# A fast matrix product whose kept weight sum moves into the tiles of the norm's rows, with weight chunks fetched three ahead

## The chip, the cores and the metric

The kernel runs on one core of a Trainium2 chip. The metric is the device time of one execution in microseconds (us); the time before is the median of three runs.

## The reference, cut to what matters

Two layers of an encoder trunk over 512 rows of width 1024. Each layer is a mixer, a cross attention and a gated MLP, each with a residual and a layer norm behind it. The change touches the MLP's second product and the norm that follows it (DFF is 2816, ALPHA is 4 to the power 1/4):

```python
def conv_ffn(x, w_up, conv_w, conv_b, w_down):
    up = x @ w_up                                  # 512 x 1024 @ 1024 x 5632
    a, g = up[..., :D_FF], up[..., D_FF:]
    g = causal_dwconv(g, conv_w) + conv_b
    return (jax.nn.gelu(g) * a) @ w_down           # 512 x 2816 @ 2816 x 1024

x = layer_norm(alpha * x + conv_ffn(...), ln_ffn_g[layer], ln_ffn_b[layer])
```

## The kernel before, in words

**Numbers.** Every matrix product is made of three matmuls on 32-bit data split into a high and a low part (`mm3`, lines 218 to 222): high by high, high by low, low by high. So each weight chunk, 128 x 1024 numbers or 512 KB, goes through a chain: SP issues a DMA into a `raw` tile, ScalarE (ACT) casts it to the high part `wh` (line 85), VectorE (DVE) subtracts that to get the low part `wl` (line 86). These two instructions together are called a split.

**The weight stream.** `plan` lists all chunks in the order of use. `Weights.load` (line 184) first fetches until more than `AHEAD` chunks are fetched and not split, then splits the oldest. `proj_batch` and the products call `weights.done()` (a `load`) each time a chunk has been used. There are 7 `raw` tiles and 5 pairs of `wh` and `wl`. A tile framework places the instructions on the engines: each engine runs its own list in order, the lists are made by the framework's scheduler, and a tile's slot is handed on when its last reader is done. So SP issues DMAs in a fixed order, and a DMA whose `raw` slot is not free holds back all DMAs behind it.

**The MLP.** The 22 feature tiles of the hidden layer go in three groups of 8, 8 and 6 (`FFN_GROUPS`). For a group, `ffn_up` computes the hidden tiles, and then a product with the matching rows of `w_down` is added to the residual `xt`. The last group uses an ordinary product followed by the norm (`residual_norm`). The first two groups use `fast_product` (line 345), a Winograd form with 7 block products in place of 8. It needs sums of weight blocks, which POOL (GpSimd) makes while the chunks are fetched (`Weights.fast`, line 136). There are four fast products in the kernel: two groups in each of two layers.

**One fast product.** It runs over four pairs of rows, i = 0 to 3. In its first half TensorE (PE) uses, for each i, a chunk `b11b21` and half of a kept sum t1 (chunk `t1t1`, one for two i). In the second half it uses, for each i, a chunk `t2b22` and half of a kept sum t4 (chunk `t4t4`). At the end it uses the kept sums t3 (chunk `t3t3`). For a chunk `t2b22` SP fetches two `raw` tiles (rows of half 1, then of half 0 of `w_down`), and POOL runs three instructions of 128 x 512: line 162 makes t3 from the first, line 163 makes t2, line 164 makes t4. Here the four `t2b22` chunks of one product are called c0 to c3, and their two DMAs c0a and c0b to c3a and c3b. `t4t4` for c0 and c1 is T4a, that for c2 and c3 is T4b.

Line 164 is the last reader of the second `raw` tile of a chunk, so that tile's slot is free when line 164 is done.

**The tile `blocks`.** t3 of all four chunks is kept in a tile of 128 x 2048 from the pool `fpool`, which has one slot. The same slot holds the hidden blocks of `ffn_up` (`Blocks.new`, line 258), four of them one after the other in a group; each is read last by the split in `finish` (line 272). Only after the last of them can t3 be written.

**The accumulators.** In the fast product PE accumulates into X, Y and Z, two PSUM tiles each. After the first half DVE adds them to `xt` (line 354): X[0], X[1], Z[0], Z[1], Y[0], Y[1], and PE then goes on accumulating into X and Y. So PE's first matmul of the second half into Y[1] waits for the add of Y[1].

**The norm's rows.** `load_rows` (line 300) fetches gain and bias of the norm, spread over 128 partitions, into the tiles `grow` and `brow` (128 x 1024, one slot each) by a DMA on POOL's queue. `residual_norm` calls it first thing, so in the MLP the rows of `ln_ffn` lie in their tiles through all three groups.

Of the kernel before, what the change touches and what calls it, by code (L numbers as in the profile page):

```python
# [8 lines left out]
F32 = mybir.dt.float32  # L9
# [5 lines left out]
P = 128  # L15
S = 512
D = 1024
# [8 lines left out]
CH = 1024  # L26
# [1 line left out]
EPS = 1e-5  # L28
WINDOWS = (2, 4, 8, 16)
RING = 5  # L30
AHEAD = 2
FFN_GROUPS = ((0, 8), (8, 16), (16, 22))
PAD = 16

# [2 lines left out]
def kernel(ctx: ExitStack, tc: tile.TileContext, a: dict, out: bass.AP):  # L37
# [8 lines left out]
    gpool = ctx.enter_context(tc.tile_pool(name="gpool", bufs=1))  # L46
    tpool = ctx.enter_context(tc.tile_pool(name="tpool", bufs=4))
    fpool = ctx.enter_context(tc.tile_pool(name="fpool", bufs=1))
# [5 lines left out]
    def nm(s):  # L54
        uid[0] += 1
        return f"{s}{uid[0]}"

    def ps_tile():
        return pspool.tile([P, 512], F32, tag="ps", name=nm("ps"))
# [4 lines left out]
    def slot(dtype=F32R):  # L64

        return apool.tile([P, 2 * CH], dtype, tag="act", name=nm("act"))
# [9 lines left out]
    def raw_tile():  # L76
        return rpool.tile([P, CH], F32, tag="raw", name=nm("raw"))

    def blocks_tile():

        return fpool.tile([P, 2 * CH], F32, tag="blocks", name=nm("blocks"))

    def split(h, l, src):

        nc.scalar.copy(h, src)  # L85
        nc.vector.tensor_sub(l, src, h.bitcast(F32))  # L86
# [41 lines left out]
    class Weights:  # L128
# [7 lines left out]
        def fast(self, what, layer, i):  # L136

            w = a["ffn_w_down"][layer]
            half = [slice(0, 512), slice(512, CH)]

            def fetch(src):
                t = raw_tile()
                nc.sync.dma_start(t[:, : src.shape[-1]], src)
                return t

            def both(key):

                if i % 2 == 0:
                    self.kept[key] = raw_tile()
                return self.kept[key][:, half[i % 2]]  # L150

            if what == "b11b21":
                w0, w1 = fetch(w[0, i]), fetch(w[1, i][:, half[0]])
                nc.gpsimd.tensor_sub(both("t1"), w1[:, half[0]], w0[:, half[0]])  # L154
                return w0
            if what == "t2b22":
                w1, w0 = fetch(w[1, i]), fetch(w[0, i])
                if i % 4 == 0:
                    self.kept["t3"] = blocks_tile()
                t3 = self.kept["t3"][:, (i % 4) * 512 : (i % 4 + 1) * 512]  # L160
                b12 = t2 = w1[:, half[0]]
                nc.gpsimd.tensor_sub(t3, w1[:, half[1]], b12)  # L162
                nc.gpsimd.tensor_add(t2, t3, w0[:, half[0]])  # L163
                nc.gpsimd.tensor_sub(both("t4"), w0[:, half[1]], t2)  # L164
                return w1
            if what == "t3t3":
                return self.kept["t3"][:, (i % 4) * 512 : (i % 4 + 2) * 512]
            return self.kept.pop({"t1t1": "t1", "t4t4": "t4"}[what])

        def fetch(self):  # L170
            if self.loaded == len(plan):
# [12 lines left out]
        def load(self):  # L184
            while self.loaded < len(plan) and len(self.fetched) <= AHEAD:
                self.fetch()
            if self.fetched:
                raw = self.fetched.pop(0)
                w = duo("w")
                split(*(t[:, : raw.shape[-1]] for t in w), raw)  # L190
                self.ready.append(w)
# [56 lines left out]
    class Blocks:  # L248
# [8 lines left out]

        def new(self):

            f = blocks_tile().rearrange("p (b s) -> p b s", b=8)  # L260

            def finish():
                def sub(to, x, y, op=ALU.subtract):
                    nc.vector.tensor_tensor(f[:, to, :], f[:, x, :], f[:, y, :], op=op)

                sub(self.S1, self.A21, self.A22, ALU.add)
                sub(self.S2, self.S1, self.A11)
                sub(self.S3, self.A11, self.A21)
                sub(self.S4, self.A12, self.S2)
                h, l = (slot()[:, : 7 * 256].rearrange("p (b s) -> p b s", b=7) for _ in range(2))  # L270
                self.pairs.append((h, l))
                split(h, l, f[:, :7, :])

            return [f[:, self.A11 :: self.A21, :], f[:, self.A12 : self.A22 + 1, :]], finish
# [20 lines left out]
    def proj_tok(ps, act, k, t, w, kk, start, stop, cols=slice(0, 512)):  # L295
        c = slice(t * P, (t + 1) * P)
        wh, wl = (v[:, kk * 512 + cols.start : kk * 512 + cols.stop] for v in w)
        mm3(ps[:, cols], act.h(k)[:, c], act.l(k)[:, c], wh, wl, start, stop)

    def load_rows(name, layer, n, eng=nc.gpsimd):  # L300
        t = gpool.tile([P, D], F32, tag=name[-1:] + "row", name=nm("row"))
        eng.dma_start(t[:, :n], a[name][layer : layer + 1, :].to_broadcast([P, n]))
        return t[:, :n]

# [109 lines left out]
    def residual_norm(groups, wname, ln, layer, last=False, hooks={}, ahead=None):  # L414

        g, b = load_rows(f"{ln}_g", layer, D), load_rows(f"{ln}_b", layer, D)
        wi = min(layer, a[wname].shape[0] - 1)
        xT = None
        for gi, (make, k0, k1) in enumerate(groups):
            act = make()
            final = gi == len(groups) - 1
            nk = k1 - k0
            if isinstance(act, Blocks):
                fast_product(act, layer, k0 // 2, gi == 0)
                continue  # L430

            def add(t, c, ps):
                z = xt[t][:, c]
                nc.vector.scalar_tensor_tensor(z, z, ALPHA if gi == 0 else 1.0, ps, op0=ALU.mult, op1=ALU.add)


            cut = [256 if last and t == NT - 1 else 512 for t in range(NT)]
            stats = [spool.tile([P, 4, 6], F32, tag="stats", name=nm("stats")) for _ in range(NT)] if final else None

            def stat(t, c0, c1):  # L440
                for c in range(c0, c1, cut[t]):
                    nc.vector.bn_stats(stats[t][:, c // cut[t], :], xt[t][:, c : c + cut[t]])

            for n in range(2):
                if n == 0 or not final:
                    ps = [ps_tile() for _ in range(NT)]
                    for k in range(nk):
                        if gi == 0 and n == 0 and k in hooks:
                            hooks[k]()
                        if k % 2 == 0:  # L450
                            c = weights.take(wname, wi, n, (k0 + k) // 2)
                        for t in range(NT):
                            proj_tok(ps[t], act, k, t, c, k % 2, k == 0, k == nk - 1)
                        if k % 2:
                            weights.done()
                    for t in range(NT):
                        add(t, slice(n * 512, (n + 1) * 512), ps[t])
                        if final:
                            stat(t, 0, 512)
                    continue  # L460
                chunks = [weights.take(wname, wi, n, (k0 + k) // 2) for k in range(0, nk, 2)]
                xT = None if last else Act(KD)
                if ahead:
                    ahead()
                for t in range(NT):
                    for c in range(0, 512, cut[t]):
                        ps = ps_tile()
                        for k in range(nk):
                            if k == 2 and c == 0 and t in (2, 3) and not last:
                                to_feat(xT, t - 2)  # L470
                            proj_tok(ps, act, k, t, chunks[k // 2], k % 2, k == 0, k == nk - 1, slice(c, c + cut[t]))
                        add(t, slice(512 + c, 512 + c + cut[t]), ps[:, c : c + cut[t]])
                        stat(t, 512 + c, 512 + c + cut[t])
                    normalise(xt[t], stats[t][:, : D // cut[t], :], g, b, (out[0, t * P : (t + 1) * P, :] if last else None))
                weights.done(len(chunks))

        def late():
            to_feat(xT, NT - 2)
            to_feat(xT, NT - 1)

        return xT, late


    def mixer_ab(xT):
# [3 lines left out]
        for k in range(KD):  # L488
# [4 lines left out]
            if k % 2:  # L493
                weights.done()
        g, b = load_rows("sgu_ln_g", 0, AW, nc.sync), load_rows("sgu_ln_b", 0, AW, nc.sync)
        for t in range(NT):
            nc.scalar.activation(v[t], ps[t], AF.Gelu_apprx_tanh)
# [314 lines left out]
```

## Time and profile before

| what | value |
|---|---|
| median of 3 runs | 1358.01 us (1357.94 to 1358.12) |
| the profiled execution, its own time | 1357.58 us |
| its span (first to last instruction) | 1355.8 us |
| mean granted TensorE clock | 0.998 of full speed |
| PE busy | 1329.4 us, 98% |
| DVE, ACT, POOL busy | 826.3, 496.9, 151.1 us |

The execution takes 1.8 us more than its span, and 0.43 us less than the median. A busy PE is not PE at its peak: a matmul of 512 columns is shown with 0.39 us, but the next one starts 0.23 us after it. Lost time of PE is therefore read from the starts of its matmuls.

### The profile page before, as it was taken

The page shows a single profiled execution, that of the slowest core. Times are in us where ns is not written, and L with a number is a line of the kernel's source. Part 1 is how long each engine was busy: PE and PEld are TensorE (multiplying, and loading weights), DVE is VectorE, ACT ScalarE, POOL GpSimd, SP SyncE. Part 2 cuts the span into 40 slices and gives each one's busy share as a digit, 9 for nine tenths or more (in the row PEclk, how much of TensorE's full clock was granted, in tenths as well). Part 3 has the DMA queues.
Part 4 walks back from the last instruction along what each step waited for, and adds up shares of the span by engine and source line. Part 5 has one row for each costly group of instructions (what it writes and reads, how often), then busy time and mean ns, then how long its engine had stood idle before and what let it go on. Part 6 is the DMA issues. An engine that isn't in the chain of part 4 may idle for free.

```text
span 1355.8 us, 16402 instructions
## 1 busy us (share of the span) xinstructions
PE 1329.4 (98%) x6526; PEld 1124.3 (83%) x6526; DVE 826.3 (61%) x1102; ACT 496.9 (37%) x671; POOL 151.1 (11%) x132
## 2 busy tenths in 40 slices
PE   8999999999999999999999999999999999999997
PEld 7888888898878887888988888988898878887886
DVE  6668446676566656547744447565676665557446
ACT  5343445235333333332522222354243333334330
POOL 0102000010150005000100001000111050213001
PEclk9999999999999999999999999999999999999999
DMA  9543533223244225433633331542152353226201
GB/s 342 181 125 98 172 120 124 62 94 109 94 162 149 86 88 181 128 95 107 202 94 97 105 94 47 159 152 78 47 156 81 104 178 120 82 92 215 94 0 63
DMA packets 47454, 161.88 MB, mean 119 GB/s; under 512 B 5648, under 2 KB 5776, under 8 KB 47376
## 3 DMA queue, kind: packets, MB, share of 16 engines
q1 hardware_dynamic: 45648, 154.53, 35.6%
q0 software_dynamic: 1728, 6.29, 1.5%
q8 instruction: 51, 0.84, 0.3%
q14 instruction: 27, 0.22, 0.1%
HBM read 158.70 MB, written 2.10 MB: 119 GB/s over the span
## 4 chain that ended last, share of the span: by engine, by line
PE 83%; issue 8%; POOL 5%; DMA 2%; DVE 1%; ACT 1%; POOLq 0%; DVEq 0%; SPq 0%
PE ps L220 27%; PE ps L221 27%; PE ps L222 27%; DMA raw<-in_ffn_w_down 2%; POOL blocks L162 2%; POOL raw L163 1%; PE ps L339 1%; POOL raw L164 1%; ACT wh L85 1%; PE ps L659 1%; POOL raw L154 0%; DVE wl L86 0%; POOL rs L311 0%; DVE x L314 0%; PE ps L536 0%
## 5 line engine op out<-in xcount | busy, mean ns | idle before, releaser
L86 DVE TENSOR_TENSOR wl<-raw,wh 128x1024 fp32r<-128x1024 f32 (+1 forms) x267 | 332.2, 1244 | 319.1 <-ACT wh L85 310.9
L85 ACT CAST wh<-raw 128x1024 fp32r<-128x1024 f32 (+1 forms) x267 | 279.0, 1045 | 551.0 <-PE ps L221 265.4
L220 PE MATMUL ps<-act,wh 128*128 128x512 f32 (+1 forms) x1316 | 478.5, 364 | 0.0
L221 PE MATMUL ps<-act,wh 128*128 128x512 f32 (+1 forms) x1316 | 478.1, 363 | 0.0
L222 PE MATMUL ps<-act,wl 128*128 128x512 f32 (+1 forms) x1316 | 478.0, 363 | 0.0
L221 PEld LDWEIGHTS ps<-act,wh 128*128 128x128 f32 x1316 | 248.4, 189 | 38.9
L220 PEld LDWEIGHTS ps<-act,wh 128*128 128x128 f32 x1316 | 248.3, 189 | 38.8
L222 PEld LDWEIGHTS ps<-act,wl 128*128 128x128 f32 x1316 | 248.3, 189 | 38.7
L220 PE MATMUL ps<-wh,act 128*128 128x512 f32 (+1 forms) x678 | 264.3, 392 | 10.6 <-DVE x L354 5.7
L221 PE MATMUL ps<-wl,act 128*128 128x512 f32 (+1 forms) x678 | 263.9, 389 | 5.9 <-DVE wl L86 5.9
L222 PE MATMUL ps<-wh,act 128*128 128x512 f32 (+1 forms) x678 | 263.6, 389 | 0.0
L220 PEld LDWEIGHTS ps<-wh,act 128*128 128x128 f32 x678 | 127.6, 189 | 39.2 <-DVE x L354 7.3
L221 PEld LDWEIGHTS ps<-wl,act 128*128 128x128 f32 x678 | 127.9, 189 | 33.8 <-DVE wl L86 8.1
L222 PEld LDWEIGHTS ps<-wh,act 128*128 128x128 f32 x678 | 127.7, 188 | 26.1
L311 POOL TENSOR_TENSOR rs<-rs,mhalf 128x1 f32<-128x1 f32 x28 | 39.9, 1427 | 808.5 <-DVE rs L310 808.5
L85 ACT CAST act<-ps 128x256 fp32r<-128x256 f32 (+1 forms) x144 | 62.9, 470 | 120.3 <-PE ps L339 79.2
L86 DVE TENSOR_TENSOR act<-ps,act 128x256 fp32r<-128x256 f32 (+1 forms) x144 | 73.0, 535 | 13.4 <-ACT act L85 13.0
L563 DVE SCALAR_TENSOR_TENSOR tmp<-ps,convw,tmp 128x511 f32<-128x511 f32 x88 | 65.6, 746 | 1.5
L700 ACT ACTIVATE tmp<-tmp 128x512 f32<-128x512 f32 x44 | 27.9, 633 | 96.9 <-DVE tmp L563 96.7
L154 POOL TENSOR_TENSOR raw<-raw,raw 128x512 f32<-128x512 f32 x16 | 26.0, 1625 | 254.7 <-DVE wl L86 202.8
L705 DVE TENSOR_TENSOR blocks<-tmp,ps 128x512 f32<-128x512 f32 x32 | 22.0, 687 | 46.3 <-PE ps L222 40.3
L86 DVE TENSOR_TENSOR act<-blocks,act 128x1792 fp32r<-128x1792 f32 x16 | 33.5, 2092 | 22.6 <-ACT act L85 22.6
(77 smaller groups left out, 778.8 us busy)
## 6 DMA issues: line engine op xcount, KB each, us to landing
raw<-in_ffn_w_up SPq DMA_DIRECT2D x88, 512.0 KB, 3.8
raw<-in_ffn_w_down SPq DMA_DIRECT2D x60, 512.0 KB, 3.5
raw<-in_c_w_in SPq DMA_DIRECT2D x24, 512.0 KB, 3.6
raw<-in_xa_wk SPq DMA_DIRECT2D x16, 512.0 KB, 3.7
raw<-in_xa_wq SPq DMA_DIRECT2D x16, 512.0 KB, 4.0
raw<-in_xa_wv SPq DMA_DIRECT2D x16, 512.0 KB, 3.6
raw<-in_xa_wo SPq DMA_DIRECT2D x16, 512.0 KB, 4.4
raw<-in_ab_w_f SPq DMA_DIRECT2D x8, 512.0 KB, 6.9
```

Source lines behind the costliest of these rows:

```text
L85: nc.scalar.copy(h, src)
L86: nc.vector.tensor_sub(l, src, h.bitcast(F32))
L154: nc.gpsimd.tensor_sub(both("t1"), w1[:, half[0]], w0[:, half[0]])
L162: nc.gpsimd.tensor_sub(t3, w1[:, half[1]], b12)
L163: nc.gpsimd.tensor_add(t2, t3, w0[:, half[0]])
L220: nc.tensor.matmul(ps, lh, rh, start=start, stop=False, skip_group_check=more)
L221: nc.tensor.matmul(ps, lh, rl, start=False, stop=False, skip_group_check=more)
L222: nc.tensor.matmul(ps, ll, rh, start=False, stop=stop, skip_group_check=more)
L311: nc.gpsimd.tensor_tensor(rs, rs, mhalf, op=ALU.pow)
L563: nc.vector.scalar_tensor_tensor(dst[:, s:], src[:, : S - s], tap(2 - s), dst[:, s:], op0=ALU.mult, op1=ALU.add)
L700: nc.scalar.activation(g, g, AF.Gelu_apprx_tanh)
L705: nc.vector.tensor_mul(to[m % 2], *halves)
```

## The change

It has three parts. (1) t3 is kept in row tiles: c0 and c1 in one of them (`grow`), c2 and c3 in the other (`brow`); the tile `blocks` is left to the hidden blocks. (2) `load_rows` moves from the head of `residual_norm` to the last group, behind `ffn_up`, since the row tiles hold t3 until then; where there is one group only, the place is the same. (3) `AHEAD` is 3 in place of 2.

```diff
-AHEAD = 2
+AHEAD = 3
...
-    def blocks_tile():
-        return fpool.tile([P, 2 * CH], F32, tag="blocks", name=nm("blocks"))
+    def row_tile(tag):
+        return gpool.tile([P, D], F32, tag=tag + "row", name=nm("row"))
...
             if what == "t2b22":
                 w1, w0 = fetch(w[1, i]), fetch(w[0, i])
-                if i % 4 == 0:
-                    self.kept["t3"] = blocks_tile()
-                t3 = self.kept["t3"][:, (i % 4) * 512 : (i % 4 + 1) * 512]
+                if i % 2 == 0:
+                    self.kept["t3", i // 2] = row_tile("gb"[i // 2 % 2])
+                t3 = self.kept["t3", i // 2][:, half[i % 2]]
...
-            if what == "t3t3":
-                return self.kept["t3"][:, (i % 4) * 512 : (i % 4 + 2) * 512]
-            return self.kept.pop({"t1t1": "t1", "t4t4": "t4"}[what])
+            return self.kept.pop({"t1t1": "t1", "t4t4": "t4", "t3t3": ("t3", i // 2)}[what])
...
-            f = blocks_tile().rearrange("p (b s) -> p b s", b=8)
+            f = fpool.tile([P, 8, 256], F32, tag="blocks", name=nm("blocks"))
...
     def load_rows(name, layer, n, eng=nc.gpsimd):
-        t = gpool.tile([P, D], F32, tag=name[-1:] + "row", name=nm("row"))
+        t = row_tile(name[-1:])
...
-        g, b = load_rows(f"{ln}_g", layer, D), load_rows(f"{ln}_b", layer, D)
         wi = min(layer, a[wname].shape[0] - 1)
         xT = None
         for gi, (make, k0, k1) in enumerate(groups):
...
                 fast_product(act, layer, k0 // 2, gi == 0)
                 continue
+            if final:
+                g, b = load_rows(f"{ln}_g", layer, D), load_rows(f"{ln}_b", layer, D)
```

The scheduler decides where the instructions stand. DVE, around the turn from the first to the second half of the first fast product, before: the splits are those of c0 (`raw_3186`), c1 (`raw_3237`), T4a (`raw_3193`), c2 (`raw_3270`), c3 (`raw_3300`) and T4b (`raw_3276`); the rows with `x_113` to `x_116` are the adds, the last one (`ps_3216`) that of Y[1].

```order
L86 TENSOR_TENSOR wl_3267<-raw_3186,wh_3266 128x1024
L354 SCALAR_TENSOR_TENSOR x_113<-x_113,ps_3217 128x512
L354 SCALAR_TENSOR_TENSOR x_114<-x_114,ps_3218 128x512
L354 SCALAR_TENSOR_TENSOR x_113<-x_113,ps_3213 128x512
L354 SCALAR_TENSOR_TENSOR x_114<-x_114,ps_3214 128x512
L86 TENSOR_TENSOR wl_3279<-raw_3237,wh_3278 128x1024
L86 TENSOR_TENSOR wl_3308<-raw_3193,wh_3307 128x1024
L354 SCALAR_TENSOR_TENSOR x_115<-x_115,ps_3215 128x512
L86 TENSOR_TENSOR wl_3330<-raw_3270,wh_3329 128x1024
L354 SCALAR_TENSOR_TENSOR x_116<-x_116,ps_3216 128x512
L86 TENSOR_TENSOR wl_3334<-raw_3300,wh_3333 128x1024
L86 TENSOR_TENSOR wl_3364<-raw_3276,wh_3363 128x1024
```

DVE at the same place in the changed kernel, where c0 to c3 are `raw_3154`, `raw_3191`, `raw_3262`, `raw_3275`, T4a is `raw_3161`, T4b is `raw_3269`, and Y[1] is `ps_3219`:

```order
L86 TENSOR_TENSOR wl_3272<-raw_3154,wh_3271 128x1024
L86 TENSOR_TENSOR wl_3283<-raw_3191,wh_3282 128x1024
L86 TENSOR_TENSOR wl_3305<-raw_3161,wh_3304 128x1024
L352 SCALAR_TENSOR_TENSOR x_113<-x_113,ps_3220 128x512
L352 SCALAR_TENSOR_TENSOR x_114<-x_114,ps_3221 128x512
L352 SCALAR_TENSOR_TENSOR x_113<-x_113,ps_3216 128x512
L352 SCALAR_TENSOR_TENSOR x_114<-x_114,ps_3217 128x512
L352 SCALAR_TENSOR_TENSOR x_115<-x_115,ps_3218 128x512
L86 TENSOR_TENSOR wl_3327<-raw_3262,wh_3326 128x1024
L86 TENSOR_TENSOR wl_3331<-raw_3275,wh_3330 128x1024
L352 SCALAR_TENSOR_TENSOR x_116<-x_116,ps_3219 128x512
L86 TENSOR_TENSOR wl_3363<-raw_3269,wh_3362 128x1024
```

The splits of c1 and T4a moved ahead of all six adds, and the add of Y[1], which stood behind the split of c2, now stands behind that of c3.

SP, the eight DMAs of c0 to c3 of the first fast product with the engines whose semaphores each waits for, before (DMAHW are semaphores of earlier DMAs):

```order
L143 DMA raw_3186<-in_ffn_w_down 128x1024 [waits DMAHW5_49,DMAHW4_49,Pool_49]
L143 DMA raw_3188<-in_ffn_w_down 128x1024 [waits DVE_49]
L143 DMA raw_3237<-in_ffn_w_down 128x1024 [waits DMAHW7_49,DVE_49]
L143 DMA raw_3239<-in_ffn_w_down 128x1024 [waits DMAHW1_49,DVE_49]
L143 DMA raw_3270<-in_ffn_w_down 128x1024 [waits DMAHW3_49,DVE_49]
L143 DMA raw_3272<-in_ffn_w_down 128x1024 [waits DVE_49]
L143 DMA raw_3300<-in_ffn_w_down 128x1024 [waits DMAHW5_49,DVE_49,Pool_49]
L143 DMA raw_3302<-in_ffn_w_down 128x1024 [waits DMAHW0_49,Pool_49]
```

SP at the same place in the changed kernel:

```order
L143 DMA raw_3154<-in_ffn_w_down 128x1024 [waits DMAHW5_49,DMAHW4_49,Pool_49]
L143 DMA raw_3156<-in_ffn_w_down 128x1024 [waits DVE_49]
L143 DMA raw_3191<-in_ffn_w_down 128x1024 [waits DMAHW7_49,DMAHW6_49,Pool_49]
L143 DMA raw_3193<-in_ffn_w_down 128x1024 [waits DVE_49]
L143 DMA raw_3262<-in_ffn_w_down 128x1024 [waits DMAHW1_49,DMAHW0_49,Pool_49]
L143 DMA raw_3264<-in_ffn_w_down 128x1024 [waits DVE_49]
L143 DMA raw_3275<-in_ffn_w_down 128x1024 [waits DMAHW3_49,DMAHW2_49,Pool_49]
L143 DMA raw_3277<-in_ffn_w_down 128x1024 [waits DVE_49]
```

c1a and c2a waited for a DVE split and now wait for POOL. In the built program c1a has the slot that c0b gives back, c2a that of c1b, and c3a that of c2b: each waits for line 164 of the chunk before it. c1b, c2b and c3b wait for the splits of the first kept t1, of the `b11b21` chunk i = 2, and of the second t1.

## Rows read from the trace of the kernel before

**Rows 1.** The page: busy time of the engines in us, with the share of the span and the instructions.

```profile
PE 1329.4 (98%) x6526; PEld 1124.3 (83%) x6526; DVE 826.3 (61%) x1102; ACT 496.9 (37%) x671; POOL 151.1 (11%) x132
```

**Rows 2.** The waits of PE over the whole span, its two rows that do not belong to the start: line, whom it waited for, us in total, times, longest us.

```profile
PE ps L221 <- DVE wl L86: 5.9, 4, 1.5
PE ps L220 <- DVE x L354: 5.7, 4, 1.4
```

**Rows 3.** The timeline of PE at the turn of the first fast product: start, us, line, what, and idle time before with its releaser.

```profile
392.96 0.39 PE L222 MATMUL ps<-wh,act 128*128 128x512 f32 x1
393.42 0.73 PE L220 MATMUL ps<-wh,act 128*128 128x512 f32 x2
395.64 0.50 PE L221 MATMUL ps<-wl,act 128*128 128x512 f32 x1 [1.48 <-DVE wl L86]
395.98 0.40 PE L222 MATMUL ps<-wh,act 128*128 128x512 f32 x1
...
398.04 0.39 PE L220 MATMUL ps<-wh,act 128*128 128x512 f32 x1
399.84 0.50 PE L220 MATMUL ps<-wh,act 128*128 128x512 f32 x1 [1.42 <-DVE x L354]
400.19 0.40 PE L221 MATMUL ps<-wl,act 128*128 128x512 f32 x1
...
401.82 0.39 PE L220 MATMUL ps<-wh,act 128*128 128x512 f32 x1
```

**Rows 4.** Busy time of the engines in one stretch of 58 us at each of the four fast products, the first and the last of the four, in the order PE, weight loads, DVE, ACT, POOL, with the granted clock and the share of the DMA engines.

```profile
347.00:405.00 58.00, 55.02 (x240) 44.57 (x239) 33.63 (x37) 21.77 (x23) 20.66 (x14) 1.00 0.40 124
...
1177.00:1235.00 58.00, 55.03 (x241) 44.56 (x240) 33.52 (x37) 21.63 (x22) 20.80 (x14) 1.00 0.37 124
```

**Rows 5.** The waits of all engines over the whole span, one row of them.

```profile
POOL blocks L162 <- DVE act L86: 115.0, 4, 28.9
```

**Rows 6.** The timeline of POOL in the first fast product: lines 162 and 163 for c0, and line 163 for c2.

```profile
383.27 1.29 POOL L162 TENSOR_TENSOR blocks<-raw 128x512 f32<-128x512 f32 x1 [28.70 <-DVE act L86]
384.64 1.29 POOL L163 TENSOR_TENSOR raw<-blocks,raw 128x512 f32<-128x512 f32 x1
...
394.58 2.15 POOL L163 TENSOR_TENSOR raw<-blocks,raw 128x512 f32<-128x512 f32 x1
```

**Rows 7.** The timeline of ACT at the same place: the cast of c2.

```profile
396.77 1.05 ACT L85 CAST wh<-raw 128x1024 fp32r<-128x1024 f32 x1 [3.40 <-POOL raw L163]
```

**Rows 8.** The timeline of DVE in the first fast product: splits of hidden blocks (1792 columns), splits of chunks (1024 columns) and adds.

```profile
358.85 2.03 DVE L86 TENSOR_TENSOR act<-blocks,act 128x1792 fp32r<-128x1792 f32 x1 [1.76 <-ACT act L85]
365.96 1.22 DVE L86 TENSOR_TENSOR wl<-raw,wh 128x1024 fp32r<-128x1024 f32 x1
371.12 1.22 DVE L86 TENSOR_TENSOR wl<-raw,wh 128x1024 fp32r<-128x1024 f32 x1 [3.95 <-ACT wh L85]
379.57 1.22 DVE L86 TENSOR_TENSOR wl<-raw,wh 128x1024 fp32r<-128x1024 f32 x1 [0.71 <-ACT wh L85]
381.16 2.03 DVE L86 TENSOR_TENSOR act<-blocks,act 128x1792 fp32r<-128x1792 f32 x1 [0.37 <-ACT act L85]
397.85 1.34 DVE L86 TENSOR_TENSOR wl<-raw,wh 128x1024 fp32r<-128x1024 f32 x1 [1.67 <-ACT wh L85]
399.11 0.68 DVE L354 SCALAR_TENSOR_TENSOR x<-x,ps 128x512 f32<-128x512 f32 x1
```

**Rows 9.** The timeline of SP: the issues of c0a, c0b and c3a, and from the view of their line the time from issue to landing of the eight DMAs of c0 to c3 (first) and of the eight that follow them in a burst (second).

```profile
354.59 0.33 SPq L143 DMA_DIRECT2D raw<-in_ffn_w_down  x1
356.32 0.33 SPq L143 DMA_DIRECT2D raw<-in_ffn_w_down  x1
388.45 0.33 SPq L143 DMA_DIRECT2D raw<-in_ffn_w_down  x1
DMA to landing us min/median/max: 3.4/3.6/4.5
DMA to landing us min/median/max: 3.6/4.7/5.7
```

**Rows 10.** The timeline of DVE and POOL at one place in the first `ffn_up`, where the two work at the same time.

```profile
339.04 2.31 DVE L86 TENSOR_TENSOR wl<-raw,wh 128x1024 fp32r<-128x1024 f32 x1
337.18 3.09 POOL L154 TENSOR_TENSOR raw<-raw,raw 128x512 f32<-128x512 f32 x1 [6.97 <-DMA raw<-in_ffn_w_down]
```

**Rows 11.** The timeline of PE at the end of the first half: its last matmul with the `b11b21` chunk i = 3, and its last with the second t1.

```profile
390.24 0.39 PE L222 MATMUL ps<-wh,act 128*128 128x512 f32 x1
391.60 0.39 PE L222 MATMUL ps<-wh,act 128*128 128x512 f32 x1
```

**Rows 12.** What lies behind the moved loads: the splits of t3 in the second fast product (timeline of DVE), the first use of the rows of `ln_ffn` in layer 0 (its line, with duration and first and last start), and the time to landing of these two row loads.

```profile
534.32 2.35 DVE L86 TENSOR_TENSOR wl<-blocks,wh 128x1024 fp32r<-128x1024 f32 x2
L312 DVE SCALAR_TENSOR_TENSOR x<-x,mv,row x4: 1274/1278/1278, 634.1 to 652.8; 128x1024 f32<-128x1024 f32 x4
DMA to landing us min/median/max: 5.2/5.5/5.8
```

**Rows 13.** What is fetched between the chunks in layer 0: the memory of the cross attention (timeline of SP), and the first product with it (timeline of PE).

```profile
81.32 6.18 SPq L90 DMA_DIRECT2D raw<-in_memT  x2
124.04 0.28 PE L220 MATMUL ps<-act,wh 128*128 128x256 f32 x1
```

## The prediction

> **What bounds the kernel now.** I read the page first: PE is busy 98% [rows 1], so only time that PE itself loses is worth anything. The list of PE's waits then says where: apart from the start, PE waits in two places, four times each, for a split (5.9 us in all) and for an add of line 354 (5.7 us) [rows 2]. Line 354 stands in `fast_product` only, and there are four fast products, so every one of them stalls twice. The stretches around them show the same busy time of PE to 0.01 us and a full granted clock [rows 4]: what holds for the first product holds for all.
>
> The timeline of PE sizes the loss better than the waits do, because matmul ends are modelled. Back to back, matmuls start 0.227 us apart (six from 390.24 to 391.60 [rows 11]). From 392.96 to 401.82 PE starts 22 matmuls [rows 3], which should take 22 x 0.2275 = 5.0 us and take 8.86. So a product loses 3.86 us at its turn, four lose 15.4 us. The parts: about 0.2 before 393.42, 1.76 before 395.64, 1.57 before 399.84, and a tenth after each restart (395.64 to 395.98 is 0.34). The rest of the span is the start, the tail behind the last matmul, and matmuls at full rate.
>
> Why it stalls: POOL's line 162 for c0 starts only at 383.27, after 28.7 us idle, released by DVE's split of the last hidden blocks [rows 6], which began at 381.16 and took 2.03 [rows 8]. This is the wait for the slot of `blocks`, 115.0 us in four times [rows 5]. Its data had long been there: c0a and c0b were issued at 354.59 and 356.32 and land after some 3.6 us [rows 9]. From 383.27 on POOL does twelve instructions without a pause, late all the way. ACT's cast of c2 starts at 396.77, at the end of POOL's t2 for c2 (394.58 + 2.15) [rows 6, 7]; DVE's split of c2 is done at 399.19, the add of Y[1] behind it starts at 399.11 and ends at 399.79 [rows 8], and PE goes on at 399.84 [rows 3].
>
> **The change part by part.** *t3 in row tiles.* POOL no longer waits for the hidden blocks. Line 162 for c0 can start when c0a lands: 354.59 + 3.6 = 358.2, which is 25 us earlier. That alone would remove 15.4 us. What is late next decides the rest, and I follow it in the first product. PE, and with it every split up to c0, keeps its times of before, since nothing stalls PE earlier.
>
> *What PE needs.* After the change PE does nine matmuls (Z[0] and Z[1] with T4a, Y[0] with c0) behind 392.96 + 0.23 = 393.19 before the first into Y[1]: that one is due at 393.19 + 9 x 0.2275 = 395.24. Its add now stands behind the splits of c2 and c3 on DVE, before only behind c2. PE sets the earliest time of these: the cast of c2 needs the weight pair of the `b11b21` chunk i = 3, last used by the matmul at 390.24, so 390.7 to 391.75 (1.05 as in [rows 7]); the cast of c3 needs that of the second t1, last used at 391.60 [rows 11], so 392.05 to 393.1. Then DVE: c2 from 391.8 to 393.0, c3 from 393.15 to 394.4 (1.22 each), the add to 395.0 (0.68) [rows 8]. That is 0.2 us early: without any disturbance the second stall is gone too, by a hair.
>
> *POOL's chain.* Three of the four pieces now fetch their first tile when POOL's line 164 of the piece before has ended, so POOL and SP take turns. Three POOL instructions take 3 x 1.37 = 4.1 us from start to start (383.27 to 384.64 is 1.37) [rows 6] when DVE leaves them alone. It does not always: at 337.18 a POOL instruction takes 3.09 in place of 1.29 beside a DVE split, and DVE's next split takes 2.31 in place of 1.22 behind it [rows 10]. Each waits for the other to end, at most a whole instruction. [...]
>
> c0: start 358.2; DVE's block split at 358.85 (2.03) and the split that follows it fall into it, so its end is between 362.3 and 365.6. c1a is issued then, and c1b waits for the split of 365.96 anyway, done at 367.2; it lands at 370.8, and lines 163 and 164 end between 373.5 and 374.7 (the split at 371.12 is in the way). c2a and c2b are issued at 374 and 374.4; c2a lands at 377.6, c2b a little over a microsecond behind it, 379. From 379 to 385 DVE wants the splits of 379.57 (1.22), of the blocks at 381.16 (2.03) and of c0 [rows 8], all paced by PE, and POOL wants two instructions. Without a meeting line 164 of c2 ends at 381.8, with all at 385.3. I take 385.3: at this density they can hardly miss each other. c3a is issued then, where before it went at 388.45, and lands at 388.9, c3b at 390.3; line 163 of c3 ends at 391.7, just in time for its cast at 392.05, but line 164 runs from 391.8 to 393.0, exactly when DVE wants the split of c2. DVE loses up to 2.31 - 1.22 = 1.09 there [rows 10], and the add of Y[1] ends at 395.95 in place of 395.0. PE stalls 395.24 to 396.0, about 0.75, plus 0.1 for the restart: a residue of 0.85 us for a product.
>
> *The row loads.* The four splits of t3 that free the row tiles end at 536.7 (534.32 + 2.35), the loads land at most 5.8 us after their issue, and the rows are first read at 634.1 [rows 12]. POOL has nothing else in its list between. Cost nothing; the cover is 90 us of the last group. If it were gone, the norm would wait up to 5.8 us, once a layer.
>
> *Three ahead.* In the plain stages it changes no split, since DMAs go when a slot is free and not when they are listed. It puts one more chunk in front of each other load on SP. The closest case I see is the memory for the cross attention, issued from 81.32 to 87.5: one chunk later is some 5 us later, and the first product with it is at 124.04 [rows 13]. Cost nothing. In the fast product it gives the new order of the adds, which is in the sum.
>
> *The sum*, against the profiled execution's own 1357.58: minus 4 x 3.86 = 15.4, plus 4 x 0.85 = 3.4, is 1345.6. The median of the runs is 0.43 above that execution, so 1346.0.
>
> **The rivals.**
> 1. *All of it goes:* line 164 of c2 ends nearer 381.8, POOL is through with c3 before 391.8, and the add is in time. 1358.0 - 15.4 = 1342.6. For it: it needs only 1.3 us of luck. Against it: the dense stretch after 379.
> 2. *The second stall stays at about its size:* the turns of POOL and SP take longer. If the DMAs of a pair land as in a burst, 4.7 in place of 3.6 [rows 9], c2 and c3 lose 1.1 each; line 163 of c3 then ends at 393.9, cast to 395.0, split to 396.2, add to 396.9, stall 1.7 with restart 1.8. Time 1342.6 + 7.2 = 1349.8; one more meeting on the way makes 2.9 and 1354.2.
> 3. *Slower:* one mechanism, the same chain over its edge. The add of Y[1] is now behind c3, the last piece. If line 163 of c3 ends after about 396.7, the stall is above 4.5 a product, more than the 3.86 of before and the bound of measurement together; at 398 it is 5.8, time 1342.6 + 23.2 = 1365.8. It needs c3a to be issued 5 us later than I think, at 390.3, later than the 388.45 of before. Nothing in the rows is that slow.
> 4. *It does nothing:* the slots of `raw` and not `blocks` would hold POOL. Time 1358. Against it: c0's data lay there for 25 us [rows 6, 9]; but c2 and c3 are held by slots, and that is rival 2.
>
> **How the numbers follow.** The forecast (residue 0.3 to 1.6 a product, 1343.8 to 1349.0) has 0.55, rival 1 0.2, rival 2 0.17, rival 3 0.04, rival 4 0.04. About 0.2% (2.7 us) is what a measurement of this kernel can tell from no change. Faster by more than that takes a residue under 3.2: the forecast, rival 1 and nearly all of rival 2, 0.91; within it, rival 4 and the end of rival 2, 0.05; slower 0.04. The range reaches from rival 1 with a little for the profile's 0.1 us, 1342.3, to rival 2 with the burst, rounded up, 1351.0; beyond it lie the end of rival 2 and rivals 3 and 4.
>
> **What would show it.** In the changed profile: POOL's wait for DVE's block split is gone, and line 162 for c0 starts near 358; SP issues c3a near 385; PE's wait for a split at the turn is gone; a wait of PE for line 352 (the add) is left four times, with 0.5 to 1 us each, and DVE's split of c2 just before it takes about 2.2. Lines 162 to 164 meet DVE splits and grow to 2 or 3 us. The loads of `ln_ffn` show no wait of DVE behind them. I am wrong if the residue is a wait for a split, if the add waits for a DMA of c3 by more than 2 us, or if PE waits in a plain stage, where I say that three ahead costs nothing.

## The result, and the profile after

| what | before | after |
|---|---|---|
| median | 1357.97 us (1357.10 to 1358.12, 4 runs) | 1346.78 us (1346.52 to 1347.30, 4 runs) |
| the profiled execution, own time / span | 1357.58 / 1355.8 us | 1347.3 / 1345.5 us |

The changed kernel takes 0.9917 of the time (95% interval 0.9905 to 0.9929): 11.2 us less. The forecast was 1346.0, the range 1342.3 to 1351.0. The lines of `fast_product` and `mm3` now have numbers smaller by two: 218 to 220 are the matmuls, 352 is the add.

The page of the changed kernel, its busy times (for [rows 1]), and the list of waits, first the two rows of PE, then two of POOL:

```profile
PE 1327.2 (99%) x6526; PEld 1125.0 (84%) x6526; DVE 838.0 (62%) x1102; ACT 497.4 (37%) x671; POOL 151.8 (11%) x132
...
PE ps L218 <- ACT wh L85: 4.7, 1, 4.7
PE ps L218 <- DVE x L352: 3.6, 4, 2.0
...
POOL row L162 <- DMA raw<-in_ffn_w_down: 59.9, 16, 4.1
POOL raw L163 <- DMA raw<-in_ffn_w_down: 14.1, 9, 2.5
```

Of the two stalls in [rows 2] the wait for a split is gone, and 3.6 us are left of waiting for an add; the 4.7 us are the start. POOL's 115.0 us of waiting for the slot of `blocks` [rows 5] has no row any more. POOL now waits for its data; before, those of c0 had been lying there for 25 us.

The timeline of POOL in the first product, the pieces c0, c2 (its last instruction) and c3 (for [rows 6]); the two issues of c3 on SP's timeline (for [rows 9]); DVE's splits of c2 and c3 and the add of Y[1] (for [rows 8]); and PE at the turn (for [rows 3]):

```profile
358.60 1.29 POOL L162 TENSOR_TENSOR row<-raw 128x512 f32<-128x512 f32 x1 [3.79 <-DMA raw<-in_ffn_w_down]
382.54 2.96 POOL L164 TENSOR_TENSOR raw<-raw,raw 128x512 f32<-128x512 f32 x1
...
390.57 1.30 POOL L163 TENSOR_TENSOR raw<-row,raw 128x512 f32<-128x512 f32 x1
391.95 1.29 POOL L164 TENSOR_TENSOR raw<-raw,raw 128x512 f32<-128x512 f32 x1
...
385.52 0.33 SPq L143 DMA_DIRECT2D raw<-in_ffn_w_down  x1
385.90 0.42 SPq L143 DMA_DIRECT2D raw<-in_ffn_w_down  x1
...
392.17 2.16 DVE L86 TENSOR_TENSOR wl<-raw,wh 128x1024 fp32r<-128x1024 f32 x1
394.25 1.21 DVE L86 TENSOR_TENSOR wl<-raw,wh 128x1024 fp32r<-128x1024 f32 x1
395.38 0.68 DVE L352 SCALAR_TENSOR_TENSOR x<-x,ps 128x512 f32<-128x512 f32 x1
...
395.21 0.39 PE L220 MATMUL ps<-wh,act 128*128 128x512 f32 x1
396.11 0.50 PE L218 MATMUL ps<-wh,act 128*128 128x512 f32 x1 [0.51 <-DVE x L352]
396.45 0.39 PE L219 MATMUL ps<-wl,act 128*128 128x512 f32 x1
```

This is the forecast chain. Line 162 of c0 starts at 358.60 in place of 383.27; line 164 of c2 ends at 385.50; SP issues c3a 0.02 us later; line 164 of c3 starts at 391.95, just before DVE's split of c2, and that split takes 2.16 in place of 1.22. The add ends at 396.06, and PE, due at 395.44, starts at 396.11: 0.67 us late, and 0.11 more at the restart.

The second and third product lose 0.70 and 0.71. The fourth loses 2.19, and here is the timeline of PE, then of POOL, then DVE's split of c2, then SP at that place, then two rows of line 143 (durations in ns and time to landing in us, min/median/max), and the DMA queues from 1206 to 1208 (packets, MB, share of the engines):

```profile
1216.26 0.39 PE L220 MATMUL ps<-wh,act 128*128 128x512 f32 x1
1218.68 0.50 PE L218 MATMUL ps<-wh,act 128*128 128x512 f32 x1 [2.03 <-DVE x L352]
...
1214.07 1.50 POOL L163 TENSOR_TENSOR raw<-row,raw 128x512 f32<-128x512 f32 x1 [2.47 <-DMA raw<-in_ffn_w_down]
1215.66 1.29 POOL L164 TENSOR_TENSOR raw<-raw,raw 128x512 f32<-128x512 f32 x1
...
1213.21 1.22 DVE L86 TENSOR_TENSOR wl<-raw,wh 128x1024 fp32r<-128x1024 f32 x1
...
1206.94 1.53 SPq L143 DMA_DIRECT2D raw<-in_ffn_w_down  x1
...
L143 SPq DMA_DIRECT2D raw<-in_ffn_w_down x64: 327/328/1526, 319.7 to 1206.9; - x64
...
DMA to landing us min/median/max: 2.5/3.6/7.0
...
q8 instruction: 1, 0.02, 4.0%
```

The issue of c3b takes 1.53 us, the only one of 64 that is long; its data land 7.0 us after the start of the issue (4.5 in the first product), POOL waits 2.47 us for them, and the whole chain is 1.5 us later. So this stall is not the collision of the other three: DVE's split of c2 runs undisturbed in 1.22 us, before line 164 starts, and what comes late is line 163, the cast and the split of c3. A packet of the queue that the page calls `instruction` (q8) is moved in the same two microseconds.

So 4.3 us of stalls are left, 4.7 with some 0.1 for each restart, where [rows 3] has 15.4 in four products. The difference of 10.7 answers to the 10.3 us by which the profiled span fell.

### The profile page after: what moved, and what is told of

Same layout as the page of the kernel before. It is cut to its first block, busy times and chain, and to the rows that moved or that the text cites. A ratio compares the mean times of both kernels' runs of the same rounds, so it can differ in the third digit from the quotient of the medians.

```text
span 1345.5 us, 16401 instructions
## 1 busy us (share of the span) xinstructions
PE 1327.2 (99%) x6526; PEld 1125.0 (84%) x6526; DVE 838.0 (62%) x1102; ACT 497.4 (37%) x671; POOL 151.8 (11%) x132
## 4 chain that ended last, share of the span: by engine, by line
PE 96%; DVE 2%; DMA 1%; issue 1%; POOL 0%; ACT 0%; POOLq 0%; DVEq 0%
PE ps L218 31%; PE ps L219 31%; PE ps L220 31%; PE ps L337 1%; DVE wl L86 1%; DMA raw<-in_ffn_w_down 1%; PE ps L658 1%; POOL rs L309 0%; DVE x L352 0%; DVE x L312 0%; PE ps L535 0%; DMA raw<-in_xT 0%; DVE stats L441 0%; DVE x L433 0%; ACT wh L85 0%
## 5 line engine op out<-in xcount | busy, mean ns | idle before, releaser
L86 DVE TENSOR_TENSOR wl<-raw,wh 128x1024 fp32r<-128x1024 f32 (+1 forms) x267 | 339.9, 1275 | 291.3 <-ACT wh L85 283.1
L86 DVE TENSOR_TENSOR act<-blocks,act 128x1792 fp32r<-128x1792 f32 x16 | 38.3, 2395 | 21.4 <-ACT act L85 21.2
```

## The experiments

The theory (A): POOL's wait for the slot of `blocks` was the one cause of both stalls of before; the residue is the add of Y[1] behind the split of c3, made late by line 164 of c3 that meets the split of c2. The rivals are named in each expectation.

**One part alone, from both sides.** `AHEAD = 2` in the changed kernel (the diff below), and `AHEAD = 3` in the kernel before (its reverse):

```diff
-AHEAD = 3
+AHEAD = 2
```

> The changed kernel with AHEAD = 2 as before; t3 stays in the row tiles and the row loads stay in the last group. Theory A (the gain comes from POOL, which no longer waits for the slot of blocks, and the order of the adds follows from that): the same time as the changed kernel, 1346.8 within 0.7 us, with four stalls of PE on the add of line 352 of about 0.7 us. Rival B, as the prediction put it (three ahead gives the new order of the adds): the add of Y[1] stands behind the split of c2 alone again; by the working of the prediction it then ends at about 394.7 even if that split meets a POOL instruction, PE is due at 395.24, and the time is 1346.8 - 4 x 0.8 = 1343.6.

Measured: 1345.98 us (1345.36 to 1347.21), stalls 3.2 us in four, the longest 1.5. That is 0.8 us less than with three ahead, but the ranges overlap, and the adds stand in the same order on DVE. Rival B, which is the prediction's own sentence on the order of the adds, is out.

> The kernel before with AHEAD = 3 alone; t3 stays in blocks, the row loads at the head of the norm. Theory A: no instruction of the fast products moves on PE, DVE, ACT or POOL, and the time is 1357.9 within 0.7 us. Rival B (three ahead gives the order of the adds and a part of the gain): faster by 1 to 3 us.

Measured: 1358.01 us, 1.0002 of before (0.9993 to 1.0011). Three ahead alone does nothing; the row tiles, with the row loads moved out of their way, do all of it, the order of the adds included.

**The adds first, in the kernel before.**

```diff
-                weights.done()
-            weights.done()
+                if not e:
+                    weights.done()
+            if i + 2 < n:
+                weights.done()
         for p in halves:
             add(p, 0, X[p])
...
             add(p + 2, 1, Y[p])
+        weights.done(2)
```

> The kernel before, with t3 in blocks and two ahead, and only the adds moved: the last two calls of weights.done() of the first half stand behind the six adds, so that the add of Y[1] no longer stands behind the split of c2. Theory A (both stalls of before have one cause, POOL starts its twelve instructions only when the slot of blocks is free): the stall of 1.57 us on the add goes, but PE only comes earlier to the second kept sum T4b, whose split ends at 405.40 and which PE before first used at about 405.6, so the stall goes there: 1357.9 within 1 us. Rival F (the order on DVE is a loss of its own): 1357.9 - 4 x 1.67 = 1351.2.

Measured: 1357.88 us, 0.9999 of before (0.9990 to 1.0008). The waits of PE (the first row holds the four stalls of 1.5 us at T4a, which stay; the second the 4.7 us of the start), and PE later in the first product:

```profile
PE ps L221 <- DVE wl L86: 7.5, 7, 1.5
PE ps L220 <- ACT wh L85: 6.4, 4, 4.7
...
403.54 0.39 PE L222 MATMUL ps<-wh,act 128*128 128x512 f32 x1
404.48 0.74 PE L220 MATMUL ps<-wh,act 128*128 128x512 f32 x2 [0.55 <-ACT wh L85]
405.74 0.50 PE L221 MATMUL ps<-wl,act 128*128 128x512 f32 x1 [0.53 <-DVE wl L86]
```

No wait for an add is left, and the time is the same: in three products PE stands at T4b instead, for its cast and its split (0.71 and 0.80 us in the first). In the second product it does not, since its clock had fallen to 0.51 (see the last section), and the product takes as long as the others. With POOL late, whatever PE gains at one wait it loses at the next. This is what makes the 15.4 us one loss and not two.

**Line 164 of c3 taken off POOL.**

```diff
-                nc.gpsimd.tensor_sub(both("t4"), w0[:, half[1]], t2)
+                t4 = both("t4")
+                if i % 4 == 3:
+                    nc.sync.dma_start(t4, w[0, i][:, half[1]])
+                else:
+                    nc.gpsimd.tensor_sub(t4, w0[:, half[1]], t2)
```

> The changed kernel, but for the last piece of each fast product (c3) POOL's line 164 is left out: its half of the second kept sum is fetched by a DMA of 256 KB from w_down, so this half is not the sum that the reference needs. All instructions of DVE, ACT and PE keep their order. Theory A (the residue is the collision of line 164 of c3 with DVE's split of c2): that split takes 1.22 us again, the add of Y[1] is about 1.0 us earlier, and the stall of about 0.8 us is gone in every product: 1346.8 - 4 x 0.8 = 1343.6. Rival C (the residue comes from c3 being late by itself, through its fetch, line 163 and its cast): DVE's split of c3 still starts when its cast is done, the stall stays and the time is 1346.8.

Measured: 1343.30 us (1342.39 to 1347.41). DVE's split of c2, the add of Y[1], and the waits of PE (lines four higher):

```profile
392.48 1.22 DVE L86 TENSOR_TENSOR wl<-raw,wh 128x1024 fp32r<-128x1024 f32 x1
394.83 0.68 DVE L356 SCALAR_TENSOR_TENSOR x<-x,ps 128x512 f32<-128x512 f32 x1
...
PE ps L222 <- ACT wh L85: 4.8, 1, 4.8
PE ps L222 <- DVE x L356: 0.3, 1, 0.3
```

The split takes 1.22 us in place of 2.16, and the stall is gone in three products and 0.3 in the fourth. The instructions of DVE and ACT stand in the same order as in the changed kernel, so in the first three products the collision is shown to make the residue; c3's fetch and line 163 were in time by themselves. For the fourth this run shows nothing: its stall had another cause, a long issue, and here no issue of line 143 took more than 0.42 us. Why one of the four runs took 1347.41 is not known. Between the two runs the 0.94 us of the split come and go with the POOL instruction.

**The adds first, in the changed kernel.** The diff is that of the experiment on before.

> The changed kernel with the last two calls of weights.done() of the first half moved behind the six adds, so that the adds stand ahead of the splits of c2 and c3 on DVE. Theory A: the add of Y[1] runs as soon as its last matmul (391.4) allows, ends at about 392.9, PE is due at 395.24, and the stall is gone; the splits of c2 and c3 become 1 to 2 us later, but PE needs c2 only some 8 us after the turn. 1346.8 - 4 x 0.8 = 1343.6. Rival D (a stall at the turn only moves on, as POOL is late for all that follows): PE waits for the split of c2, c3 or the second kept sum instead, and the time is 1346.8 or more.

Measured: **1342.03 us** (1341.75 to 1342.58), 0.9885 of before (0.9870 to 0.9899), 4.7 us less than the changed kernel and the fastest here. The waits of PE, all of its rows, and the adds on DVE:

```profile
PE ps L218 <- ACT wh L85: 4.8, 1, 4.8
...
388.52 3.85 DVE L352 SCALAR_TENSOR_TENSOR x<-x,ps 128x512 f32<-128x512 f32 x6
392.29 1.65 DVE L86 TENSOR_TENSOR wl<-raw,wh 128x1024 fp32r<-128x1024 f32 x1
```

Only the start is left. The six adds run in one piece to 392.37, the collision is still there (the split of c2 takes 1.65), and it costs nothing. The adds themselves, which read one input from PSUM, did not collide: in this run they took 0.64 us each, and POOL's lines 162 and 163 of c3 beside them 1.29 and 1.30. The expectation of 1343.6 took 0.8 for each product; the 4.7 us measured are the three stalls of 0.7, the one of 2.2 and the restarts. Against before it is 15.9 us, for the 15.4 read from [rows 3].

**One raw tile fewer.**

```diff
-    rpool = ctx.enter_context(tc.tile_pool(name="rpool", bufs=7))
+    rpool = ctx.enter_context(tc.tile_pool(name="rpool", bufs=6))
```

> The changed kernel with 6 raw tiles in place of 7. Theory A (POOL and SP take turns over raw slots, and the chain of c0 to c3 ends only just too late): every fetch waits for a later release, c0a goes about 3 us later and c3a some 2 to 4 us later than at 385.5, and nothing of that is hidden, so the residue grows by 2 to 4 us in each product: 1355 to 1363, about as long as before the change. Rival E (the slots are not what spaces the pieces; the collisions of POOL and DVE do): within 1 us of 1346.8.

Measured: 1375.21 us (1373.64 to 1375.99), 1.0125 of before (1.0108 to 1.0142), 28 us more than the changed kernel, far above the 1355 to 1363 of theory A. The two issues of c3 on SP, line 163 of c3 on POOL, PE at the turn, and the engines in stretches of the first product (the column behind POOL is the granted clock):

```profile
391.20 0.81 SPq L143 DMA_DIRECT2D raw<-in_ffn_w_down  x2
...
396.15 2.12 POOL L163 TENSOR_TENSOR raw<-row,raw 128x512 f32<-128x512 f32 x1
...
396.28 0.39 PE L220 MATMUL ps<-wh,act 128*128 128x512 f32 x1
401.35 0.79 PE L218 MATMUL ps<-wh,act 128*128 128x512 f32 x1 [4.68 <-DVE x L352]
401.94 0.63 PE L219 MATMUL ps<-wl,act 128*128 128x512 f32 x1
402.37 0.63 PE L220 MATMUL ps<-wh,act 128*128 128x512 f32 x1
...
390.00:396.00 6.00, 5.70 (x25) 4.43 (x25) 6.00 (x8) 1.06 (x1) 2.40 (x2) 1.00 0.62 219
401.00:406.00 5.00, 4.65 (x11) 3.68 (x12) 1.52 (x2) 1.04 (x1) 0.00 (x0) 0.50 0.81 311
406.00:412.00 6.00, 6.00 (x27) 4.87 (x27) 2.45 (x2) 2.10 (x2) 0.00 (x0) 0.98 0.31 87
```

The direction is as expected: c3a goes out 5.7 us later than at 385.52, and the stall on the add is 4.84 us. What was not expected stands behind it. Matmuls start 0.43 us apart and not 0.23, at a granted clock of 0.50, after PE had stood still from 396.5 to 401.35. Until it is back at 0.98 PE loses another 2.4 us (up to 2.7 in the other products). So a product loses some 7.7 us: 0.4 at a first small stall, 4.9 and 2.4. Four of them less the 4.7 of the changed kernel are 26 of the 28 us; followed matmul by matmul, the four turns hold 27.2 of the 28.7 us by which the profiled span is longer.

**Six raw tiles, and the adds first.** Both diffs together, on the changed kernel.

> Six raw tiles as in the run with 1375 us, and the adds ahead of the last splits as in the run with 1342 us. Theory A (a late c3 costs only through the add of Y[1] behind its split): the stall of 4.8 us and the low clock behind it are gone; the first, small stall of that run (0.33 to 0.45 us, the adds behind splits that POOL holds up) may stay: 1342 + 4 x 0.4 = 1343.6. Rival G (the pieces themselves are too late for PE with six slots): PE waits for a split of c2, c3 or T4b instead, and the time is above 1350.

Measured: 1345.38 us (1344.97 to 1346.28). PE's waits, all but the start:

```profile
PE ps L218 <- DVE x L352: 0.7, 4, 0.2
```

Six tiles cost 28 us in the order of the changed kernel, and 3.4 us (against 1342.03) with the adds first. Of these, a small stall at X[0] takes 0.33 a product and 0.1 at the restart, 1.8 in all. Followed matmul by matmul against the run with 1342.03, whose profiled span is 3.2 us shorter, the rest is no stall at a turn: 0.4 come at the start, and 1.0 behind the last matmul, from which the span's end is 11.3 us away with six tiles, in this run and the one before, and 10.2 with seven. c3a goes out at 390.35, nearly as late as in the run before. So a late c3 hurt only through the add behind its split.

**One raw tile more.**

```diff
-    rpool = ctx.enter_context(tc.tile_pool(name="rpool", bufs=7))
+    rpool = ctx.enter_context(tc.tile_pool(name="rpool", bufs=8))
...
-    tpool = ctx.enter_context(tc.tile_pool(name="tpool", bufs=4))
+    tpool = ctx.enter_context(tc.tile_pool(name="tpool", bufs=2))
```

> The changed kernel with 8 raw tiles in place of 7; for the room, the tmp tiles are 2 in place of 4, which moves some instructions of the first mixer and none of the fast products. Theory A1, as the prediction has it (POOL and SP take turns over the raw slots, this makes c3 late): with a slot more c3a is issued some 3 us earlier than at 385.5, line 164 of c3 is done before DVE splits c2, the residue goes, and the time is 1342. Theory A2 (what costs is where POOL's instructions meet DVE's splits, and being earlier moves them to a worse place): line 162 to 164 of c3 then run from about 381 to 386, while DVE splits c0, c1 and T4a back to back; three meetings cost up to 1.09 each, the adds of X start up to 3.3 us later where they have some 2 us to spare, and both X[0] and Y[1] stall: 1346.8 + 4 x 2.2 = 1355.6.

Measured: 1354.29 us (1353.15 to 1355.06), 7.5 us more than with 7. The waits of PE; SP's issues of c3; POOL's three instructions for c3; DVE's splits of c0, c1 and T4a, and the first add; and PE's two stalls in the first product:

```profile
PE ps L218 <- DVE x L352: 9.4, 8, 1.5
...
380.86 0.80 SPq L143 DMA_DIRECT2D raw<-in_ffn_w_down  x2
...
384.37 2.15 POOL L162 TENSOR_TENSOR row<-raw 128x512 f32<-128x512 f32 x1 [3.54 <-DMA raw<-in_ffn_w_down]
386.59 2.15 POOL L163 TENSOR_TENSOR raw<-row,raw 128x512 f32<-128x512 f32 x1
388.82 2.16 POOL L164 TENSOR_TENSOR raw<-raw,raw 128x512 f32<-128x512 f32 x1
...
385.28 6.78 DVE L86 TENSOR_TENSOR wl<-raw,wh 128x1024 fp32r<-128x1024 f32 x3
391.99 0.68 DVE L352 SCALAR_TENSOR_TENSOR x<-x,ps 128x512 f32<-128x512 f32 x1
...
392.81 0.47 PE L218 MATMUL ps<-wh,act 128*128 128x512 f32 x1 [1.03 <-DVE x L352]
397.97 0.50 PE L218 MATMUL ps<-wh,act 128*128 128x512 f32 x1 [1.49 <-DVE x L352]
```

c3 is fetched 4.7 us earlier and POOL is done with it at 390.98, before DVE splits c2. By the prediction's rival 1, which asks for that before 391.8, nothing should be left. But the three instructions now meet three splits in a row, which take 6.78 us, where three at 1.22 would be 3.7; the first add starts 2.9 us later than with 7 tiles, and both X[0] and Y[1] wait. Read from the starts, the eight stalls are 10.7 us, with the restarts 11.5, where 7 tiles leave 4.7: 6.8 of the 7.5 us. What the two `tmp` tiles cost elsewhere was not measured apart. Theory A2, not A1.

## Why the prediction was right

*What PE loses before.* 15.4 us from [rows 3]; the run without any stall at the turn is 15.9 below before. That both stalls have one cause was taken from the rows. Two runs show it: the row tiles alone (two ahead) take away the first stall and, in three products, half of the second, and putting the adds first in the kernel before only moves the second stall on.

*POOL's chain.* 358.2 against 358.60 for its start; 385.3 against 385.50 for line 164 of c2; 385.3 against 385.52 for c3a; 391.8 against 391.95 for line 164 of c3. The choice of the upper bound at c2 was right. So was the reading that DVE and POOL wait for each other's whole instruction: line 164 of c2 took 2.96 in place of 1.29, and the split of the hidden blocks that it met 2.96 in place of 2.03. One link in between lies outside its bounds: line 164 of c1 ended at 375.09, where at most 374.7 was given, and c2a could be used from 378.88 in place of 377.6. It did not matter: line 164 of c2 waited for DVE's split of the hidden blocks, which ran from 381.38 to 384.34.

*The residue.* 0.85 a product was forecast; three products have 0.67 to 0.71 and some 0.1 for the restart. The cause in these three is as forecast, and shown by taking line 164 of c3 away. **The term that was off** is the fourth product, 2.19: the prediction let c3b land 1.4 us behind c3a four times. There one of its own signs of being wrong did show, an add that waits for a DMA of c3 by more than 2 us: POOL waits 2.47 us for c3b, and the add is late by it. The prediction's sum has 3.4 us of residue where the trace has 4.7; that 1.3 is more than the whole miss of 0.8. With 4.7 the sum gives 1346.9 for the profiled execution, which took 1347.3; but the median, which the prediction put 0.43 above the profiled execution, is 0.5 below it. The two misses partly cancel, so that the forecast comes as near as 0.8 is partly luck. Whether the long issue comes from the packet of q8 is not shown. The same DMA has a long issue in two other profiles, of 1.01 us with two ahead and of 1.24 with the adds first.

*Three ahead.* That it costs nothing in the plain stages holds. That "in the fast product it gives the new order of the adds" was wrong: with two ahead the order is the same. The order comes with the row tiles. It did not touch the sum, which used the order and not its reason.

*The row loads.* Nothing: no row of the waits has DVE or PE behind the loads of `ln_ffn`.

*The rivals.* Rival 1's condition, POOL through with c3 before 391.8, is not enough for its time: with a c3 fetched at 380.86 it was met, and the time was 1354.3. That run has c3 4.7 us earlier; the 1.3 us of which the rival speaks were not tried. Its time (1342.6) was reached another way, by putting the adds first. Only the fourth product came near rival 2 (1.8 a product), and not by its burst: one landing took 7.0 us. Rival 3 was right about where the edge is, and priced it too low: with a stall of 4.8 us the clock was lost too, each time, so that its 5.8 us would have been about 8 (an estimate: 5.8 and the 2.4 to 2.7 measured there).

## What to carry to other kernels

When a stall is found, follow the chain past it before pricing its removal: the add of Y[1] and T4b were both late from one slot, so that putting the adds first was worth nothing before the slot was freed (1357.88) and 4.7 us after (1342.03). When small work stands behind large work on an in-order engine and a third engine waits for the small one, put it first: this made a whole `raw` tile nearly unnecessary, while a tile more (with two `tmp` tiles fewer) made things worse. Earlier was not better where DVE and POOL held each other up (with 8 `raw` tiles three splits took 6.78 us in place of 3.7); look at what the moved instructions will meet.

## What the runs showed of the hardware

With six `raw` tiles a stall had a second price. Behind 4.8 us of standing still PE ran at half its clock (0.50) for 4.9 to 5.6 us, 2.4 to 2.7 us lost on top; the mean granted clock of that execution was 0.987, against 0.998 before. The same came after less: in the second product of the run with the adds first in the kernel before, a stall of 1.5 us was followed by this (PE's timeline, and the granted clock behind POOL's column):

```profile
524.84 0.63 PE L221 MATMUL ps<-wl,act 128*128 128x512 f32 x1 [1.49 <-DVE wl L86]
525.27 0.63 PE L222 MATMUL ps<-wh,act 128*128 128x512 f32 x1
...
525.00:528.00 3.00, 3.00 (x8) 2.32 (x9) 1.95 (x3) 1.04 (x1) 2.92 (x3) 0.51 0.26 105
```

Its three other products, with the same stall, kept the full clock (the mean of that execution was 0.997). The product took no longer for it: the clock cost some 1.6 us, and PE then no longer stood waiting for T4b.

In the ten profiles 13 DMA issues on SP behind the first 10 us took longer than 0.6 us, 0.8 to 1.6 in place of 0.33; the data of the one of 1.53 us landed 2.5 us later than those of its like in the first product (7.0 in place of 4.5). Each of the 13 starts within 0.6 us of a 16 KB packet of q8, of which a run has 51: before, the only one, 1.22 us at 26.79, starts 0.25 us behind such a packet, and in the changed kernel the only one, at 1206.94, 0.12 us. Most such packets passed without a long issue, and the cause was not tested.
